# Seven-product couples first in a pair and plain couples last, the second halves' first up chunk in program order, and scratch tiles of their own for the last squares

## The chip, the cores and the metric

The kernel runs on one core of a Trainium2 chip. The metric is the time of one execution on the device, in microseconds (us). The kernel before takes 2386.35 us (median of 3 runs, 2380.95 to 2389.92). An execution under the hardware profiler gives the trace from which all other times come.

Names of the engines: PE is TensorE's matmul, PEld its load of weights, DVE the vector engine, ACT the scalar engine, POOL GpSimd, SP the engine whose queue issues most transfers. PSUM is the memory with 8 banks into which TensorE sums; SBUF is the large on-chip memory; a DMA moves data between the chip's main memory and SBUF.

## The reference, cut to what matters

Two layers over 256 tokens of width 2048. Each is a normed token mixer (an mLSTM in layer 0, an HGRN2 in layer 1) and a normed gated FFN, both added to the stream h. A last norm closes. The change lies in the FFN's second product and in what follows it:

```python
def conv_glu(hn, w_up, conv_w, conv_b, w_down):
    u = hn @ w_up                        # 2048 -> 2 x 5504
    a, v = jnp.split(u, 2, axis=-1)
    ...                                  # c = conv_b + 3-tap convolution of a along the tokens
    return (jax.nn.gelu(c, approximate=False) * v) @ w_down      # 5504 -> 2048

for layer in range(DEPTH):
    ...
    h = h + mix
    h = h + conv_glu(rmsnorm(h, norm_ffn_g[layer]), ...)
return rmsnorm(h, final_g)
```

## The kernel before, in words

**Precision.** The weights lie in main memory as fp32. A piece of 128 x 1024 is loaded ("raw"), split by ACT into a rounded part wh (L149) and by DVE into the rest wl (L150), and every block product is three matmuls: high x high, high x low, low x high. So ACT and DVE work on every weight, and TensorE waits for both.

**The FFN.** Its 5504 hidden columns are worked in two parts per layer, of 22 and 21 blocks of 256 columns: an "up" phase of 22 (21) chunks of some 11 us (matmuls L338 and L342), and then two "pairs", each of which multiplies the whole part into half of the 2048 output columns. After a chunk, done_up (L1184 to L1196) adds up the PSUM banks on ACT and DVE, convolves, applies the GELU and leaves a tile g of 128 hidden columns with its high and low part.

**A pair** (squares_by_seven, matmuls L236) takes two tiles g at a time, a "couple". A plain couple is 24 matmuls on two pieces of weights. A "seven" couple computes the same 2 x 2 blocks by Strassen's scheme with 7 products: 21 matmuls on three and a half pieces. The products P1, P5, P6, P7 collect in four PSUM banks of the pool psm (tag mm, four buffers, the same that the up chunks use), the rest in four banks of pc. The scheme needs sums of blocks of weights (a tile T of 128 x 1536) and sums of tokens (sx). The sums of weights are made ahead, during the up phase, and put into main memory (tscr); in the pair they are loaded (L199), except for one couple, FLY, whose sums DVE makes itself (L208). The sums of tokens are made by token_sums (L564 to L569) as soon as both tiles g are there. SEVEN names the couples of a part that go by seven products.

**What sets the order.** A scheduler fills the engines' queues from priorities and dependencies; what is wrapped in pin or keep_in_program_order stays where it is written. Casts run up to three pieces ahead of the matmuls (LOOK = 3), raw has three buffers. T tiles share the three buffers of the tag avc with the temporaries of done_up. Small work of other stages (norms, preparation of sums) is pushed to a list of side jobs and taken a step at a time.

**End of a pair.** After the last seven couple, mid() (L581 to L589) adds P1, P5, P6, P7 to h, on ACT, DVE and POOL, by way of a scratch tile u of the tag jk, which has one buffer. After the last couple, done() adds the banks pc. In the second part's second pair the last couples run bank by bank (36 matmuls), and each finished bank goes straight to the next norm: to Norm.bank in layer 0, which transposes h on TensorE (L422), and to FinalNorm.bank in layer 1 (L504 to L516), whose last stores end the kernel. Its squares for output block c == 2 run on ACT (L534) and write their unused result to a scratch tile jk.

Of the kernel before, what the change touches and what calls it, by code (L numbers as in the profile page):

```python
# [8 lines left out]
F32 = mybir.dt.float32  # L9
F32R = mybir.dt.float32r  # L10
I32 = mybir.dt.int32
AF = mybir.ActivationFunctionType
# [3 lines left out]
P = 128  # L16
T = 256
# [29 lines left out]
LEAD = 48  # L47
TEMP = 3
GATES = 4 * AH
SEVEN = (1, 2, 3, 4, 5, 6, 7, 8, 9), (1, 2, 3, 4, 5, 6, 7, 8)  # L50
FLY = 5
STORED = 2 * (len(SEVEN[0]) + len(SEVEN[1]) - 2)
BY_TRANSFERS = (9, 27.0), (17, 33.0)
FIRST = 11, 7
# [12 lines left out]
def trunk_kernel(ctx, tc, xT, x_d, fg_d, pp_d, cst_d, w_gate, w_first, w_aq, w_ak, w_av, w_ao, w_aout, w_ao2,  # L67
                 w_bq, w_bv, w_bg, w_bout, w_bo2, w_up, w_d0, w_d1, out, mscr, tscr):
    nc = tc.nc
    act, dve, pool, pe = nc.scalar, nc.vector, nc.gpsimd, nc.tensor  # L70

    keep = ctx.enter_context(tc.tile_pool(name="keep", bufs=1))
# [21 lines left out]
    class Side:  # L94
        def __init__(self):
            self.now, self.jobs, self.behind = 0.0, [], []
# [26 lines left out]
    side, held = Side(), []  # L123


    class Chunk:
        def __init__(self, kind, src, nk, x, done, before=None, swap=(), first=False, paced=False):
            self.swap, self.first, self.paced = swap, first, paced
            self.kind, self.src, self.nk, self.x, self.done, self.before = kind, src, nk, x, done, before
            self.width = {"fm": 256, "tm": 512, "st": 512}[kind]  # L130

    pin = tc.keep_in_program_order
# [90 lines left out]
    def banks():  # L223
        return [psm.tile([P, 512], F32, tag="mm", name="mm") for _ in range(2)]
# [81 lines left out]
    def stream(chunks):  # L306
        pieces = split_weights(chunks)
        ready = []

        def fetch():  # L310
            p = next(pieces, None)
            if p is not None:
                ready.append(p)

        for _ in range(LOOK):
            fetch()
        for ch in chunks:
            if ch.before:
                ch.before()
            if ch.kind == "st":  # L320
                squares_by_seven(ch, fetch, ready)
                continue
            ps = banks()
            k = 0
            while k < ch.nk:
                fetch()
                wh, wl, n = ready.pop(0)
                if ch.kind == "fm":
                    ops = [(kk, f, part) for kk in range(n) for f in range(2) for part in "hl"]
                    for i in ch.swap:  # L330
                        i -= 2 * k
                        if 0 <= i < 2 * n - 1:
                            ops[2 * i + 1:2 * i + 3] = ops[2 * i + 2], ops[2 * i + 1]
                    for kk, f, part in ops:
                        x = ch.x(k + kk)
                        c = kk * ch.width + f * P
                        if part == "h":
                            pe.matmul(ps[f], wh[:, c:c + P], x, start=k + kk == 0, stop=False)  # L338
                            continue
                        if f:  # L340
                            side.tick(0.65)
                        pe.matmul(ps[f][:, 0:T], wl[:, c:c + P], x[:, 0:T], start=False, stop=k + kk == ch.nk - 1)  # L342
                    k += n
                    continue
                for kk in range(n):
                    x = ch.x(k)
                    st, sp = k == 0, k == ch.nk - 1
                    c = slice(kk * 512, (kk + 1) * 512)
                    ops = [(t, i) for t in range(2) for i in range(3)]
                    if ch.first and st:  # L350
                        ops.sort(key=lambda o: (0, 2, 1)[o[1]])
                    for t, i in ops:
                        a, w = ((0, wh), (0, wl), (T, wh))[i]
                        pe.matmul(ps[t], x[:, a + t * P:a + (t + 1) * P], w[:, c], start=st and i == 0, stop=sp and i == 2)  # L354
                    side.tick(1.3)
                    k += 1
            ch.done(ps)
# [112 lines left out]
    class FinalNorm:  # L470
# [5 lines left out]

        def load(self):
            self.g = [keep.tile([P, 512], F32, tag=f"xt{c}", name=f"fg{c}") for c in range(4)]
            for c in range(4):
                pool.dma_start(self.g[c], fg_d[:, c * 512:(c + 1) * 512].broadcast_to([P, 512]))  # L480

        def add(self, c):
            cs = slice(512 * c, 512 * c + 512)
# [15 lines left out]
        def bank(self, ps, i):  # L499
            if i == 0:  # L500
                side.drain()
            t, c = i // 2, 2 + i % 2
            h, total, rc = hm[:, t, 512 * c:512 * c + 512], self.ss[:, t, c:c + 1], self.rc[:, t:t + 1]
            pin(dve.tensor_tensor(h, h, ps, ALU.add))  # L504
            if c == 2:
                square(h, total)
                if t:
                    self.store(0)
                pin(dve.scalar_tensor_tensor(rc, total, 1.0 / D, rc, ALU.mult, ALU.add))
                return  # L510
            last = keep.tile([P, 512], F32, tag=f"xt{4 + t}", name="fl")
            pin(dve.scalar_tensor_tensor(last, h, 1.0, h, ALU.mult, ALU.mult, accum_out=total))
            pin(dve.scalar_tensor_tensor(rc, total, 1.0 / D, rc, ALU.mult, ALU.add))
            pool.tensor_tensor(rc, rc, hmx[:, 0:1], ALU.pow)
            v = hm[:, t, 1024:1536]
            pin(dve.tensor_tensor(v, v, self.g[2], ALU.mult))  # L516
            if t:
                self.store(1)
# [13 lines left out]
    def square(src, total, pin=lambda ins: ins):  # L532
        jk = ev.tile([P, 512], F32, tag="jk", bufs=1, name="jk")
        pin(act.activation(jk, src, AF.Square, accum_out=total))  # L534
# [630 lines left out]
    def ffn(layer, norm, nxt):  # L1165
# [39 lines left out]
        for part, (f0, nf) in enumerate(((0, FA), (FA, FB))):  # L1205
            GT, SX, seven = [], {}, SEVEN[part]

# [7 lines left out]
            for i in range(nf):  # L1215
                chunks.append(Chunk("fm", w_up[layer, f0 + i], KT, norm.x, done_up(f0 + i, i, GT, SX, seven),
                                    prep if i == 0 else None,
                                    swap=((2, 12), (2,))[layer] if part and i == 0 else (3,) if f0 + i == 1 else (), paced=True))

            for c0, src in ((0, w_d0[layer][:, f0 * 1024:(f0 + nf) * 1024]), (2, w_d1[layer][:, f0 * 1024:(f0 + nf) * 1024])):  # L1220
                ch = pair(src, nf, c0, lambda k, GT=GT: GT[k], lambda u, SX=SX: SX[u], nxt if part else None, seven)
                ch.waits = []
                for u in seven:
                    if u != FLY:
                        ch.stored[u] = tscr[box["n"]]
# [23 lines left out]
    nf = FinalNorm()  # L1249
    chunks = mlstm(n0, n1)  # L1250
    c, close0, chunks[6].before = ffn(0, n1, n2)
    chunks += c
    c = hgrn(n2, n3)
    b = c[0].before

    def swap():
        close0()
        b()
    c[0].before = swap
    d, close1, c[1].before = ffn(1, n3, nf)  # L1260
    chunks += c + d
    stream(chunks)
    close1()

# [97 lines left out]
```

## Time and profile before

| what | value |
| --- | --- |
| time, median of 3 runs | 2386.35 us (2380.95 to 2389.92) |
| the profiled execution | 2386.37 us, span 2384.4 us, clock 0.998 |
| TensorE busy | 2361.6 us, 14524 matmuls |
| pairs of layer 0 start at | 639.36, about 695, 986.09, about 1037 us |
| pairs of layer 1 start at | 1925.51, about 1980, 2265.97, about 2318 us |
| last matmul ends, span ends | 2372.17, 2384.4 us |

A row of the timeline gives start, duration, engine, line, operation, output <- inputs; in square brackets stands how long the engine had been idle before it, and what released it. A row of the stages gives a stretch, its length and the busy time of the engines in it. Matmuls overlap, so the time that one costs is the distance between starts (0.227 us for 128 x 512), not its duration.

### The profile page before, as it was taken

To read this page: it belongs to the slowest core of one execution; us is meant where nothing else is said; L and a number is where in the kernel's file an instruction comes from. 1 tells how busy PE (TensorE), PEld (TensorE's weight loads), DVE (VectorE), ACT (ScalarE), POOL (GpSimd) and SP (SyncE) were. 2 spreads that over 40 slices of the span, in tenths; PEclk is the share of its full clock that TensorE was granted. 3 is DMA by queue.
4 is the path that set the end of the run, shared out by engine and by line. 5 is a ranking of instruction groups with operands and counts; after the bars stand their busy time and mean duration, and the time that the engine had idled before them with its cause. 6 is when DMAs were issued, how large, how long until landed. Compare 5 with 4: busy or idle time off the path is not lost.

```text
span 2384.4 us, 38410 instructions
## 1 busy us (share of the span) xinstructions
PE 2361.6 (99%) x14524; PEld 2019.2 (85%) x14524; DVE 1998.9 (84%) x3254; ACT 1393.0 (58%) x2201; POOL 282.4 (12%) x348
## 2 busy tenths in 40 slices
PE   9999999999999999999999999999999999999997
PEld 7888888888888888888888888888888888888876
DVE  7766677988899888898898989889779889888888
ACT  7655455555565555676555555556556576455565
POOL 0110111000000000001333333331010000000000
PEclk9999999999999999999999999999999999999999
DMA  8766878888798888796777777767897788777785
GB/s 299 215 212 232 257 221 274 309 296 289 275 340 305 292 278 280 272 328 219 223 222 232 211 236 222 221 213 235 279 309 274 245 307 325 265 248 243 246 322 203
DMA packets 122986, 624.32 MB, mean 262 GB/s; under 512 B 13856, under 2 KB 14368, under 8 KB 74672
## 3 DMA queue, kind: packets, MB, share of 16 engines
q1 hardware_dynamic: 106128, 590.59, 70.1%
q0 software_dynamic: 16096, 30.48, 8.3%
q8 instruction: 114, 1.87, 0.3%
q10 hardware_dynamic: 576, 0.79, 0.1%
q14 instruction: 72, 0.59, 0.1%
HBM read 584.00 MB, written 92.34 MB: 284 GB/s over the span
## 4 chain that ended last, share of the span: by engine, by line
PE 85%; DVE 5%; DMA 5%; issue 2%; ACT 1%; POOL 1%; SPq 0%; POOLq 0%; DVEq 0%; ACTq 0%
PE mm L338 33%; PE mm L342 17%; PE mm L354 16%; PE pc L236 9%; PE mm L236 7%; DVE wl L150 3%; DMA raw<-in_w_up 1%; DMA T<-tscr 1%; DMA pwh<-in_w_d 1%; DMA raw<-in_w_d 1%; DMA pwl<-in_w_d 1%; PE pn L845 1%; ACT wh L149 1%; PE py L1102 1%; PE pd L1052 0%
## 5 line engine op out<-in xcount | busy, mean ns | idle before, releaser
L338 PE MATMUL mm<-xt,wh 128*128 128x512 f32 x3776 | 1317.9, 394 | 0.0
L150 DVE TENSOR_TENSOR wl<-raw,wh 128x1024 fp32r<-128x1024 f32 (+1 forms) x844 | 1033.7, 1229 | 242.9 <-ACT wh L149 237.0
L149 ACT CAST wh<-raw 128x1024 fp32r<-128x1024 f32 (+1 forms) x844 | 875.2, 1043 | 564.6 <-PE mm L338 295.7
L342 PE MATMUL mm<-xt,wl 128*128 128x256 f32 x3776 | 1051.6, 280 | 1.8 <-issue 1.2
L338 PEld LDWEIGHTS mm<-xt,wh 128*128 128x128 f32 x3776 | 705.8, 187 | 158.9
L342 PEld LDWEIGHTS mm<-xt,wl 128*128 128x128 f32 x3776 | 711.5, 188 | 7.4 <-issue 2.0
L354 PE MATMUL mm<-wh,xt 128*128 128x512 f32 x1024 | 321.7, 393 | 1.8 <-ACT xt L360 1.6
L236 PE MATMUL pc<-wh,g 128*128 128x512 f32 x696 | 237.8, 390 | 0.0
L354 PEld LDWEIGHTS mm<-wh,xt 128*128 128x128 f32 x1024 | 192.1, 188 | 42.2 <-ACT xt L360 2.1
L354 PE MATMUL mm<-wl,xt 128*128 128x512 f32 x512 | 198.7, 392 | 0.0
L236 PE MATMUL mm<-wh,sx 128*128 128x512 f32 x444 | 157.2, 389 | 0.3 <-ACT wh L149 0.3
L149 ACT CAST wh<-T 128x1024 fp32r<-128x1024 f32 (+1 forms) x148 | 122.2, 835 | 55.9 <-DMA T<-tscr 15.6
L236 PEld LDWEIGHTS pc<-wh,g 128*128 128x128 f32 x696 | 130.6, 188 | 27.2
L150 DVE TENSOR_TENSOR wl<-T,wh 128x1024 fp32r<-128x1024 f32 (+1 forms) x148 | 141.5, 967 | 13.1 <-ACT wh L149 12.8
L588 POOL TENSOR_TENSOR hm<-hm,u 128x512 f32<-128x512 f32 x10 | 14.8, 1478 | 1090.4 <-DVE u L587 813.5
L236 PE MATMUL pc<-wl,g 128*128 128x512 f32 x348 | 135.7, 390 | 0.5 <-DVE wl L150 0.5
L354 PEld LDWEIGHTS mm<-wl,xt 128*128 128x128 f32 x512 | 96.6, 189 | 19.1
L1184 ACT COPY avc<-mm 128x256 f32<-128x256 f32 x172 | 64.1, 372 | 69.4 <-PE mm L342 69.4
L236 PEld LDWEIGHTS mm<-wh,sx 128*128 128x128 f32 x444 | 83.2, 188 | 18.0 <-ACT wh L149 0.8
L236 PE MATMUL mm<-wl,sx 128*128 128x512 f32 x222 | 86.6, 390 | 0.6 <-DVE wl L150 0.6
L1189 ACT ACTIVATE avc<-avc,pp 128x256 f32<-128x256 f32 x86 | 51.6, 601 | 57.4 <-DVE avc L1187 57.4
L1185 DVE TENSOR_TENSOR avc<-mm,avc 128x256 f32<-128x256 f32 x172 | 72.2, 420 | 8.6 <-ACT avc L1184 8.4
(248 smaller groups left out, 2444.1 us busy)
## 6 DMA issues: line engine op xcount, KB each, us to landing
raw<-in_w_up SPq DMA_DIRECT2D x172, 1024.0 KB, 5.9
raw<-in_w_bq SPq DMA_DIRECT2D x48, 1024.0 KB, 5.2
raw<-in_w_d SPq DMA_DIRECT2D x60, 768.0 KB, 5.8
T<-tscr SPq DMA_DIRECT2D x60, 768.0 KB, 7.6
tscr<-in_w_d SPq DMA_DIRECT2D x26, 1024.0 KB, 7.5
raw<-in_w_ao SPq DMA_DIRECT2D x24, 1024.0 KB, 6.0
raw<-in_w_d SPq DMA_DIRECT2D x24, 1024.0 KB, 7.0
pwh<-in_w_d SPq DMA_DIRECT2D x36, 512.0 KB, 6.6
```

Source lines behind the costliest of these rows:

```text
L149: pin(act.copy(wh[:, :m], r))
L150: pin(dve.tensor_tensor(wl[:, :m], r, wh[:, :m].bitcast(F32), ALU.subtract))
L236: pin(pe.matmul(ps, a, b, start=id(ps) not in begun, stop=stop and i == 2))
L338: pe.matmul(ps[f], wh[:, c:c + P], x, start=k + kk == 0, stop=False)
L342: pe.matmul(ps[f][:, 0:T], wl[:, c:c + P], x[:, 0:T], start=False, stop=k + kk == ch.nk - 1)
L354: pe.matmul(ps[t], x[:, a + t * P:a + (t + 1) * P], w[:, c], start=st and i == 0, stop=sp and i == 2)
L588: pool.tensor_tensor(part(1, 0), part(1, 0), u, ALU.add)
L845: pe.matmul(pn[:, 0:258], w, v, start=(i == 0), stop=(i == len(parts) - 1))
L1102: pe.matmul(py[:, c], AT[:, s if s == t else 2 + s], V[:, s, j * P:(j + 1) * P], start=(s == 0), stop=(s == 1))
L1184: act.copy(z, p[:, T:2 * T])
L1185: dve.tensor_tensor(z, p[:, 0:T], z, ALU.add)
L1189: act.activation(c, a, AF.Identity, bias=col("conv_b", layer * FT + f), scale=cw[1])
```

## The change

Four edits. The first moves the couples: SEVEN now names couples 0 to 8 of a part of eleven, and 0 to 7 of the other, instead of 1 to 9 and 1 to 8; FLY is couple 4 instead of 5. A pair opens with a product couple and ends with two plain couples, mid() runs a couple earlier, and the sums of tokens are made from the first chunks of an up phase on instead of up to its last ones. The second edit gives the first up chunk of each second part another exchange of neighbouring matmuls (swap), and keeps the matmuls of its first piece in program order (hold). The third turns the final norm's weight loads on POOL (fg) into side jobs of 9.0 steps, in program order. The fourth lets the squares of FinalNorm.bank write a tile sq of their own, in place of the shared jk. Every engine has as many instructions as before.

```diff
-SEVEN = (1, 2, 3, 4, 5, 6, 7, 8, 9), (1, 2, 3, 4, 5, 6, 7, 8)
-FLY = 5
+SEVEN = (0, 1, 2, 3, 4, 5, 6, 7, 8), (0, 1, 2, 3, 4, 5, 6, 7)
+FLY = 4
...
+                    hold = pin if ch.hold and k == 0 else lambda ins: ins
                     for kk, f, part in ops:
...
-                            pe.matmul(ps[f], wh[:, c:c + P], x, start=k + kk == 0, stop=False)
+                            hold(pe.matmul(ps[f], wh[:, c:c + P], x, start=k + kk == 0, stop=False))
...
-                        pe.matmul(ps[f][:, 0:T], wl[:, c:c + P], x[:, 0:T], start=False, stop=k + kk == ch.nk - 1)
+                        hold(pe.matmul(ps[f][:, 0:T], wl[:, c:c + P], x[:, 0:T], start=False, stop=k + kk == ch.nk - 1))
...
         def load(self):
             self.g = [keep.tile([P, 512], F32, tag=f"xt{c}", name=f"fg{c}") for c in range(4)]
+            side.push(self.loads(), True)
+
+        def loads(self):
             for c in range(4):
-                pool.dma_start(self.g[c], fg_d[:, c * 512:(c + 1) * 512].broadcast_to([P, 512]))
+                yield 9.0
+                tc.keep_in_program_order(pool.dma_start(self.g[c], fg_d[:, c * 512:(c + 1) * 512].broadcast_to([P, 512])))
...
             if c == 2:
-                square(h, total)
+                sq = keep.tile([P, 512], F32, tag=f"xt{6 + t}", name="sq")
+                act.activation(sq, h, AF.Square, accum_out=total)
...
-                                    swap=((2, 12), (2,))[layer] if part and i == 0 else (3,) if f0 + i == 1 else (), paced=True))
+                                    swap=(0, 2) if part and i == 0 else (3,) if f0 + i == 1 else (), paced=True,
+                                    hold=part == 1 and i == 0))
```

Lines of the changed kernel stand a few further down: L338 is L339 there, L504 is L509, L509 is L515, and mid()'s L581 to L589 are L587 to L595.

What this does to the queues shows at three places. The first is TensorE's queue at the start of the first pair of all, before the change (mm are banks of psm, pc the other four, g tiles of hidden columns with their numbers, sx sums of tokens):

```order
3044 L236 MATMUL pc<-wh,g_3982 128x512
3045 L236 MATMUL pc<-wl,g_3982 128x512
3046 L236 MATMUL pc<-wh,g_3982 128x512
3047 L236 MATMUL pc<-wh,g_4088 128x512
3048 L236 MATMUL pc<-wl,g_4088 128x512
3049 L236 MATMUL pc<-wh,g_4088 128x512
```

And the same place after it:

```order
3044 L236 MATMUL mm<-wh,g_3982 128x512
3045 L236 MATMUL mm<-wl,g_3982 128x512
3046 L236 MATMUL mm<-wh,g_3982 128x512
3047 L236 MATMUL pc<-wh,g_3982 128x512
3048 L236 MATMUL pc<-wl,g_3982 128x512
3049 L236 MATMUL pc<-wh,g_3982 128x512
3050 L236 MATMUL mm<-wh,sx 128x512
3051 L236 MATMUL mm<-wl,sx 128x512
```

Before, 24 plain matmuls on pc come first; now product P1 on mm stands first, and the first product with a sum of tokens, which needs the first T, is the seventh matmul.

The second is SP's queue of transfers for the same pair, before:

```order
107 L137 DMA raw<-in_w_d 128x2048
108 L137 DMA raw<-in_w_d 128x1536
109 L200 DMA raw<-tscr 128x512
110 L199 DMA T<-tscr 128x1536
111 L137 DMA raw<-in_w_d 128x1536
112 L200 DMA raw<-tscr 128x512
113 L137 DMA raw<-in_w_d 128x1536
114 L200 DMA raw<-tscr 128x512
115 L137 DMA raw<-in_w_d 128x1536
116 L200 DMA raw<-tscr 128x512
117 L199 DMA T<-tscr 128x1536 x3
```

And after:

```order
107 L137 DMA raw<-in_w_d 128x1536
108 L200 DMA raw<-tscr 128x512
109 L137 DMA raw<-in_w_d 128x1536
110 L200 DMA raw<-tscr 128x512
111 L199 DMA T<-tscr 128x1536
112 L137 DMA raw<-in_w_d 128x1536
113 L200 DMA raw<-tscr 128x512
114 L137 DMA raw<-in_w_d 128x1536
115 L200 DMA raw<-tscr 128x512
116 L199 DMA T<-tscr 128x1536 x2
117 L137 DMA raw<-in_w_d 128x2048
```

The raw tile of the plain couple (128x2048, row 107 before) has gone from the front, and the second T stands behind four raw tiles instead of five.

The third is DVE's queue at the end of the last pair, before:

```order
2890 L582 TENSOR_TENSOR hm<-hm,mm 128x512
2891 L150 TENSOR_TENSOR wl<-raw,wh 128x1024
2892 L584 TENSOR_TENSOR hm<-hm,mm 128x512
2893 L586 TENSOR_TENSOR hm<-hm,mm 128x512
2894 L583 TENSOR_TENSOR u<-u,mm 128x512
2895 L585 TENSOR_TENSOR hm<-hm,u 128x512
2896 L587 TENSOR_TENSOR u<-u,mm 128x512
2897 L504 TENSOR_TENSOR hm<-hm,pc 128x512
```

And after:

```order
2873 L588 TENSOR_TENSOR hm<-hm,mm 128x512
2874 L590 TENSOR_TENSOR hm<-hm,mm 128x512
2875 L592 TENSOR_TENSOR hm<-hm,mm 128x512
2876 L150 TENSOR_TENSOR wl<-raw,wh 128x1024
2877 L589 TENSOR_TENSOR u<-u,mm 128x512
2878 L150 TENSOR_TENSOR wl<-raw,wh 128x1024 x2
2879 L591 TENSOR_TENSOR hm<-hm,u 128x512
2880 L593 TENSOR_TENSOR u<-u,mm 128x512
2881 L509 TENSOR_TENSOR hm<-hm,pc 128x512
```

Three subtractions for weights stand among mid()'s six operations instead of one; mid() itself is a couple further from the end of TensorE's work.

More of the change, by code (lines that the diff above doesn't have):

```diff
@@ L126, in trunk_kernel, with __init__ @@
     class Chunk:
-        def __init__(self, kind, src, nk, x, done, before=None, swap=(), first=False, paced=False):
-            self.swap, self.first, self.paced = swap, first, paced
+        def __init__(self, kind, src, nk, x, done, before=None, swap=(), first=False, paced=False, hold=False):
+            self.swap, self.first, self.paced, self.hold = swap, first, paced, hold
             self.kind, self.src, self.nk, self.x, self.done, self.before = kind, src, nk, x, done, before
```

## Prediction

> **What bounds the kernel now.** I read the page first, for the busy engine and the chain that ended last.
>
> ```profile
> span 2384.4 us, 38410 instructions
> PE 2361.6 (99%) x14524; PEld 2019.2 (85%) x14524; DVE 1998.9 (84%) x3254; ACT 1393.0 (58%) x2201; POOL 282.4 (12%) x348
> PE 85%; DVE 5%; DMA 5%; issue 2%; ACT 1%; POOL 1%; SPq 0%; POOLq 0%; DVEq 0%; ACTq 0%
> ```
>
> TensorE is busy for 2361.6 of 2384.4 us, and 85% of the chain that ended last is its own work. The change removes no matmul, so only moments in which TensorE waits, and the tail behind its last matmul, can change the time. All of it lies in the four parts where the FFN's second products run (two "pairs" each). The second view is the table by stage: the first pair cut in two, the first pair of layer 1, and the last two pairs. Columns: PE, PEld, DVE, ACT and POOL busy, granted clock, DMA share, GB/s.
>
> ```profile
> 639.36:650.00 10.64, 10.64 (x49) 8.59 (x47) 5.93 (x12) 4.48 (x9) 0.00 (x0) 1.00 0.84 327
> 650.00:694.00 44.00, 43.24 (x187) 34.63 (x187) 42.40 (x47) 33.35 (x39) 0.00 (x0) 1.00 0.90 339
> 1925.51:1980.00 54.49, 54.49 (x243) 45.09 (x242) 49.77 (x59) 39.86 (x48) 0.89 (x1) 1.00 0.93 348
> 2265.97:2318.00 52.03, 51.87 (x230) 42.58 (x228) 44.02 (x54) 33.48 (x42) 0.45 (x1) 1.00 0.91 331
> 2318.00:2372.20 54.20, 52.26 (x228) 42.64 (x228) 50.74 (x63) 34.36 (x45) 6.53 (x4) 1.00 0.59 215
> ```
>
> The clock is full, so no part of the time is the clock's. Inside a pair DVE is busy for 42.40 of 44.00 us and the DMA engines for 0.90 of the time: both are close behind TensorE. The first 10.64 us of a pair, where today a plain couple (24 matmuls on two pieces of weights) stands, are its only slack: DVE 5.93 us.
>
> The third view is the timeline of TensorE around the places where it stopped.
>
> ```profile
> 649.60 0.62 PE L236 MATMUL mm<-wh,sx 128*128 128x512 f32 x2
> 650.41 0.50 PE L236 MATMUL mm<-wh,g 128*128 128x512 f32 x1 [0.19 <-ACT wh L149]
> 664.05 0.50 PE L236 MATMUL pc<-wl,g 128*128 128x512 f32 x1 [0.54 <-DVE wl L150]
> 1088.22 0.55 PE L422 MATMUL mm<-cst,hm 128*128 128x128 f32 x3 [1.28 <-DVE u L587]
> 2314.55 2.00 ACT L149 CAST wh<-raw 128x1024 fp32r<-128x1024 f32 x2 [4.26 <-DMA raw<-in_w_d]
> 2319.34 0.50 PE L236 MATMUL mm<-wh,g 128*128 128x512 f32 x1 [1.50 <-ACT wh L149]
> 2320.88 0.50 PE L236 MATMUL mm<-wl,sx 128*128 128x512 f32 x1 [0.57 <-DVE wl L150]
> ```
>
> There is little to win: 0.19 in the first pair, 0.54 at the couple whose sums DVE makes itself (L208), 1.28 where the next norm's transposes want a PSUM bank that DVE's L587 of mid() has yet to read, and 1.50 + 0.57 at the start of the last pair. The last has its cause five us earlier: ACT stood 4.26 us for a weight transfer and started late. The fourth view is the timeline of the tail.
>
> ```profile
> 2368.43 1.30 POOL L589 TENSOR_TENSOR hm<-hm,u 128x512 f32<-128x512 f32 x1
> 2369.77 0.63 ACT L534 ACTIVATE jk<-hm 128x512 f32<-128x512 f32 x1 [7.54 <-POOL hm L589]
> 2370.52 0.16 DVE L509 SCALAR_TENSOR_TENSOR fss<-fss 128x1 f32<-128x1 f32 x1 [2.82 <-ACT jk L534]
> 2370.60 0.68 DVE L504 TENSOR_TENSOR hm<-hm,pc 128x512 f32<-128x512 f32 x1
> 2371.78 0.39 PE L236 MATMUL pc<-wh,g 128*128 128x512 f32 x1
> 2375.34 0.68 DVE L504 TENSOR_TENSOR hm<-hm,pc 128x512 f32<-128x512 f32 x1
> ```
>
> The last matmul ends at 2372.17 (2371.78 + 0.39), but DVE takes the last bank only at 2375.34. Behind it come 9.06 us of closing work and stores to 2384.4. DVE is late because the first square waits for POOL's L589: the square writes a scratch tile (tag jk) whose one buffer L589 still reads as u.
>
> **The change, part by part.** The profiled execution took 2386.37 us, span 2384.4, which is the median (2386.35) but for 0.02; the sum is made against it.
>
> *Last squares.* With tiles of their own, and with mid() one couple of 24 matmuls (5.4 us) earlier, the first square waits for nothing but its bank. The tail is 36 matmuls bank by bank at 0.227 us (in the timeline one starts every 0.227), so bank 2 of 4 is complete 18 matmuls, 4.08 us, before 2372.17, at 2368.09. From its L504 to that of the fourth bank the order on DVE and ACT is kept: 2375.34 - 2370.60 = 4.74 us. So the fourth L504 starts near 2368.24 + 4.74 = 2372.98, with 0.15 for the handover: **-2.4**. It cannot be better than 3.1 (TensorE's end). It is nothing if mid() now makes DVE late for the first banks.
>
> ```profile
> 2317.38 1.22 DVE L150 TENSOR_TENSOR wl<-raw,wh 128x1024 fp32r<-128x1024 f32 x1
> 2317.55 2.19 POOL L588 TENSOR_TENSOR hm<-hm,u 128x512 f32<-128x512 f32 x1 [58.66 <-DVE u L587]
> 2318.51 2.31 DVE L150 TENSOR_TENSOR wl<-T,wh 128x1024 fp32r<-128x1024 f32 x1
> ```
>
> That mishap has a row: beside POOL's L588 a subtraction of 1.22 us took 2.31, and the add 2.19 instead of 1.30. In the tail today the two adds run beside bank sums at 1.30; now they run beside subtractions. Price on DVE 2 x 1.09 = 2.2 us, within two couples (10.9 us of TensorE) that ask DVE for four subtractions (4.9) and mid()'s six operations (4.1, by the 0.68 of an L504 of the same shape): 11.2, a third of a us too much, but up to three pieces are cast ahead. The two orders of DVE in the tail, shown with the change, say the same: mid() still comes last ahead of the banks, with three subtractions in it instead of one. I take 0. The Trainium skill (SBUF — State Buffer, Who interferes with whom) says that a DVE instruction with two SBUF inputs contends with a GpSimd one that reads SBUF, and that one with a single SBUF input does not; the trace agrees (2.31 against 1.22, and 1.30 beside sums that read PSUM). By that rule alone the tail's gain would shrink by those 0.3, to -2.1.
>
> *mid() one couple earlier.* The PSUM banks of the products come free before the next norm's transposes ask for them: **-1.28** at 1088.22. At 2317 the two plain couples at the end need 2 pieces each where the seven-product couple before needed 3.5, so loads of the next pair come through earlier: **-2.07**, or nothing if the transfers themselves were the limit there (DMA share 0.91). The 0.19 of the first pair goes, the 0.54 moves with its couple and stays: **-0.19**.
>
> *Seven-product couples first.* Now the price. The two orders of TensorE at the first pair, shown with the change, open with three plain matmuls on bank pc before, and with three of a product on bank mm now. So products stand where 24 plain matmuls stood. The second sum tile T, which today is asked for after 24 + 21 matmuls, is asked for at the 28th matmul here and at the 33rd at the other three starts (counted in the order of TensorE). The rows around it now:
>
> ```profile
> 639.36 0.39 PE L236 MATMUL pc<-wh,g 128*128 128x512 f32 x1
> 641.06 0.42 DVE L1185 TENSOR_TENSOR avc<-mm,avc 128x256 f32<-128x256 f32 x1
> 641.39 0.68 DVE L150 TENSOR_TENSOR wl<-T,wh 128x512 fp32r<-128x512 f32 x1
> 642.10 0.99 SPq L199 DMA_DIRECT2D T<-tscr  x2
> 648.36 1.05 ACT L149 CAST wh<-T 128x1024 fp32r<-128x1024 f32 x1 [2.83 <-DMA T<-tscr]
> 649.32 1.04 ACT L149 CAST wh<-raw 128x1024 fp32r<-128x1024 f32 x1
> DMA to landing us min/median/max: 6.2/6.8/7.4
> ```
>
> T takes one of three buffers that it shares with the last chunks' temporaries, so its load is issued (642.10) when DVE has finished the wl before it. In the new order L1193 and L1185 stand behind that wl, so the issue moves from 642.10 to about 640.8, no earlier than 640.3 (with the other wl too) and no later than 642.1. Plus 6.2 and a cast of 1.05: 648.05. TensorE asks at 639.36 + 27 x 0.227 = 645.5. Stall 2.55; the raw piece cast behind T in ACT's order (649.32, a step of 0.96) is asked for two matmuls (0.45) later: 0.5 more. **+3.0**; bounds, with 4.2 (below) from 640.3 and 7.4 from 642.1: 0 to 5.6. For the other three starts the landings of the T loads in the first tens of us, and the first issue, are (986.09, 1925.51 and 2265.97, in this order):
>
> ```profile
> L199 SPq DMA_DIRECT2D T<-tscr x9: 319/320/451, 985.7 to 1025.3; - x9
> DMA to landing us min/median/max: 4.2/7.8/9.0
> L199 SPq DMA_DIRECT2D T<-tscr x2: 319/319/319, 1925.2 to 1928.9; - x2
> DMA to landing us min/median/max: 4.2/5.2/6.3
> L199 SPq DMA_DIRECT2D T<-tscr x5: 319/320/428, 2267.5 to 2289.9; - x5
> DMA to landing us min/median/max: 5.5/8.0/9.3
> ```
>
> The 33rd matmul comes 32 x 0.227 = 7.3 us after the start. At 986 I take the middle of the landings: 985.7 + 6.6 + 1.05 = 993.4, just in time: **0** (bounds 0 to 2.4). At 1925: 1925.2 + 5.2 + 1.05 = 1931.5, needed at 1932.8: **0** (0 to 2.5 with the 9.0 of 986). At 2266 the load waits for less in the new order than now (SP's queue only), so I put it a us earlier, 2266.5 + 7.4 + 1.05 = 2275.0 against 2273.3, and take two thirds, since the rest of that stretch has the lowest DVE load: **+1.2** (0 to 4.6).
>
> PSUM is not late: the product banks 3 and 4 wait for DVE's two L1185, which ended by 642.41, and are asked for at the 22nd and 25th matmul, 644.1 and 644.8. The sums of the last couples leave the end of each up phase, about 2.0 us of DVE, and enter its beginning, in steps of 0.29 us under chunks of some 11:
>
> ```profile
> L564 DVE TENSOR_TENSOR avc<-avc x136: 279/292/295, 453.7 to 2241.7; 128x128 f32<-128x128 f32 x136
> L480 POOL DMA_DIRECT2D fg<-in_fg x4: 536/546/615, 2256.0 to 2258.4; - x4
> ```
>
> *Up chunk kept in order, and the norm weights' loads.* At 750 and 2035 TensorE goes from pair to chunk without a wait now; a pinned order with another swap costs 0, covered by pieces cast ahead; uncovered it would be one cast, 1.05, at each of two places. The fg loads hold POOL 0.55 us each, the fourth now between two pairs' adds; DVE wants them 70 us later: 0.
>
> **Sum:** -2.4 - 1.3 - 2.1 - 0.2 = -6.0; +3.0 + 0 + 0 + 1.2 = +4.2; net -1.8: 2384.5 us.
>
> **Rivals.** (a) *The loads land in time everywhere.* Against it are the 6.2 and 8.0 above, for it the 4.2. Then only the gains count: 2386.4 - 6.0 = 2380. The Trainium skill (DMA: Bandwidth & Descriptors, Anatomy of one DMA) gives about 2.0 us and 436 GB/s for a DMA of its software path; for T's 786 KB an estimate of 3.8 us, and by it the first T would be cast at 645.7 and nothing would stall. No landing quoted here was that short.
> (b) *T starves all four starts: slower.* One mechanism: the shared buffer is freed late and the load stands behind the raw pieces on the same busy engines. At the long landings: 640.8 + 9.0 + 1.05 - 645.5 + 0.5 = 5.9 (9.0 seen at 986), 2.4, 2.5 and 4.6, together 15.4; minus 6.0: 2395.8. It decides from landings of 3.7, 6.7, 6.6 and 4.8 us on, in the order of the starts (the time asked for, less the cast and the issue), where each further us costs a us. If DVE, at 42.40 of 44.00 us, cannot catch up afterwards and the 2.1 at 2319 isn't won either, 2398.
> (c) *The gains move instead of going*: the 2.1 at 2319 (transfers at 0.91 are the limit) and the tail (DVE late from the slow subtractions) stay, and the starts cost 4.2: 2386.4 - 1.5 + 4.2 = 2389.
>
> **Chances.** Forecast 0.43, (a) 0.27, (b) 0.15, (c) 0.15. The range takes in (a) with the tail's 3.1 and (b) at its price: 2377 to 2395.5; the forecast's own is 2381 to 2388. A measurement here can tell about 0.5% (12 us) from no change, so nearly all of this is "no change": faster than 2374.4 would need twice the gains found, 0.05; slower than 2398.3 is (b) without the 2.1, 0.07; the same 0.88.
>
> **What would show it.** Right: TensorE waiting for ACT's wh, and ACT for T<-tscr, some 6 us behind 639 and little of it at 986 and 1925; no wait for L593 near 1088; the last bank's L509 about 0.8 us behind TensorE's end. Wrong: TensorE without a wait in the first 12 us of all four pairs (then a), waits over 2 us at 986 and 1925 (then b), or ACT's square still behind POOL's L595 or the start of the last pair still waiting 2 us (then c).

## The result, and the profile after

The changed kernel takes 2378.88 us (median of 20 runs, 2373.34 to 2387.07); the kernel before, on the same chip, 2385.78 (20 runs, 2380.82 to 2395.82). The ratio is 0.9972, with a 95% interval of 0.9962 to 0.9982: 6.7 us less, between 4.3 and 9.1. It is a small gain, under the 0.5% that the prediction took for the least that a measurement can tell; with 20 runs of each the interval is 0.1% to either side, so the gain is told from no change. It is larger than the 1.8 us of the forecast. The profiled execution took 2383.29 us, span 2381.3, so it is one of the slower ones of its kernel by 4.4 us; the two traces can't be subtracted as wholes, only place by place.

The page of the changed kernel, the lines that answer to those of before:

```profile
span 2381.3 us, 38367 instructions
PE 2361.4 (99%) x14524; PEld 2016.8 (85%) x14524; DVE 1998.7 (84%) x3254; ACT 1392.0 (58%) x2201; POOL 283.8 (12%) x348
PE 88%; DMA 4%; DVE 4%; issue 2%; ACT 1%; POOL 1%; SPq 0%; POOLq 0%; DVEq 0%; ACTq 0%
```

TensorE's busy time is what it was. The waits at the pairs, from TensorE's timeline of the changed kernel (the first pair begins at 638.02, the first of layer 1's second part at 2264.46, the last one near 2316.5):

```profile
644.56 0.73 PE L236 MATMUL mm<-wh,sx 128*128 128x512 f32 x2 [0.23 <-ACT wh L149]
645.51 0.50 PE L236 MATMUL pc<-wh,g 128*128 128x512 f32 x1 [0.21 <-ACT wh L149]
2273.21 0.50 PE L236 MATMUL mm<-wl,sx 128*128 128x512 f32 x1 [0.24 <-DVE wl L150]
2345.64 0.50 PE L236 MATMUL mm<-wh,g 128*128 128x512 f32 x1 [1.17 <-ACT wh L149]
```

The 1.28 us at the norm's transposes and the 1.50 + 0.57 at the start of the last pair are gone, and the 0.54 at the couple whose sums DVE makes is 0.16. A wait of 1.17 stands in the middle of the last pair instead, in this execution. At the start of the first pair TensorE waits 0.44 us, where the forecast had 3.0. The tail:

```profile
2366.19 0.63 ACT L512 ACTIVATE sq<-hm 128x512 f32<-128x512 f32 x1 [7.37 <-DVE hm L509]
2367.51 0.69 DVE L509 TENSOR_TENSOR hm<-hm,pc 128x512 f32<-128x512 f32 x1 [0.40 <-PE pc L236]
2371.16 0.39 PE L236 MATMUL pc<-wh,g 128*128 128x512 f32 x1
2372.26 0.68 DVE L509 TENSOR_TENSOR hm<-hm,pc 128x512 f32<-128x512 f32 x1
```

The square now waits for its bank's sum alone, and the last bank is taken 0.71 us behind TensorE's last matmul (2371.55), where it was 3.17. From the last matmul to the end are 9.75 us instead of 12.21.

These add up to some 6 us less, with 0.7 of new waits at the starts and 1.2 in the last pair. Layer 1's first up phase has three waits in this execution (0.60, 0.40 and 1.56 us), where before it had one of 0.48. What I had not looked at is the pace of the up phases where they have no waits. The table by stage shows it: two stretches of 200 us inside the up phases of the two second parts, and 100 us of layer 1's first part, before:

```profile
770.00:970.00 200.00, 200.00 (x1134) 173.40 (x1133) 171.04 (x281) 110.19 (x175) 0.00 (x0) 1.00 0.83 283
1810.00:1910.00 100.00, 100.00 (x579) 88.19 (x578) 84.74 (x138) 56.04 (x91) 0.00 (x0) 1.00 0.73 248
2050.00:2250.00 200.00, 200.00 (x1156) 174.83 (x1155) 168.02 (x271) 111.53 (x179) 0.00 (x0) 1.00 0.73 248
```

And of the changed kernel:

```profile
770.00:970.00 200.00, 200.00 (x1156) 174.88 (x1155) 173.01 (x283) 113.64 (x181) 0.00 (x0) 1.00 0.84 286
1810.00:1910.00 100.00, 100.00 (x568) 86.86 (x568) 82.98 (x135) 55.77 (x91) 0.00 (x0) 1.00 0.72 242
2050.00:2250.00 200.00, 200.00 (x1156) 174.90 (x1155) 167.31 (x269) 112.14 (x180) 0.00 (x0) 1.00 0.73 247
```

TensorE is busy for all of each stretch, at a granted clock of 1.00, and still gets through 1134 matmuls in one stretch of 200 us and 1156 in another. A chunk's matmuls alternate between 512 and 256 columns, so that is 200 / 567 = 353 ns for a pair of matmuls against 200 / 578 = 346. A second part's up phase has 21 x 32 = 672 such pairs: 4.5 us. Layer 0's second part ran at the slow pace before and at the fast one now. Layer 1's first part (1810 to 1910) was fast before and is slow in this execution: 579 and 568 in 100 us.

### The profile page after: what moved, and what is told of

The parts are those of the page before. It is cut to its first block, busy times and chain, and to the rows that moved or that the text cites. A ratio compares the mean times of both kernels' runs of the same rounds, so it can differ in the third digit from the quotient of the medians.

```text
span 2381.3 us, 38367 instructions
## 1 busy us (share of the span) xinstructions
PE 2361.4 (99%) x14524; PEld 2016.8 (85%) x14524; DVE 1998.7 (84%) x3254; ACT 1392.0 (58%) x2201; POOL 283.8 (12%) x348
## 4 chain that ended last, share of the span: by engine, by line
PE 88%; DMA 4%; DVE 4%; issue 2%; ACT 1%; POOL 1%; SPq 0%; POOLq 0%; DVEq 0%; ACTq 0%
PE mm L339 33%; PE mm L343 17%; PE mm L355 16%; PE pc L236 11%; PE mm L236 7%; DVE wl L150 2%; DMA T<-tscr 1%; DMA raw<-in_w_up 1%; DMA pwh<-in_w_d 1%; PE pn L851 1%; ACT wh L149 1%; PE py L1108 1%; PE pd L1058 0%; DMA pwl<-in_w_d 0%; PE pa L1058 0%
## 5 line engine op out<-in xcount | busy, mean ns | idle before, releaser
L339 PE MATMUL mm<-xt,wh 128*128 128x512 f32 x3776 | 1318.4, 396 | 0.4 <-issue 0.4
L339 PEld LDWEIGHTS mm<-xt,wh 128*128 128x128 f32 x3776 | 707.8, 188 | 161.7 <-issue 0.7
```

Of the source, the lines that this page charges most:

```text
L339: hold(pe.matmul(ps[f], wh[:, c:c + P], x, start=k + kk == 0, stop=False))
```

## Experiments

**Two theories.** M: how an up phase begins decides its pace, and the second edit, which I had costed at nothing, brings 4.5 us that way; the couples and the tail bring the rest. N: the second edit does nothing, as predicted, and the moved couples carry the whole gain.

**The second edit undone in the changed kernel.**

```diff
-                                    swap=(0, 2) if part and i == 0 else (3,) if f0 + i == 1 else (), paced=True,
-                                    hold=part == 1 and i == 0))
+                                    swap=((2, 12), (2,))[layer] if part and i == 0 else (3,) if f0 + i == 1 else (), paced=True))
```

> The changed kernel with its second edit undone: the first up chunk of each second part has its old exchanges and is not kept in program order, all else stays. Theory M (the start of an up phase decides its pace): in the changed kernel the up phase of layer 0's second part runs at about 347 ns for a pair of matmuls (128x512 and 128x256), in the kernel before at 353; the start of the chunk sets this for all 21 chunks. Undoing the edit puts one or both second up phases at another start, and if at the slow pace it costs 660 x 6.6 ns = 4.3 us each: 2383 to 2388 us, ratio to the kernel before 0.999 to 1.001. Theory N (the couples and the tail make the gain, the edit costs and brings nothing, as predicted): ratio 0.997, and 347 ns in both phases.

Measured: 2384.20 us (12 runs), ratio 0.9986 (0.9975 to 0.9997), 3.3 us over the changed kernel's ratio; the two intervals overlap, so the count of matmuls says more here. The two second up phases:

```profile
770.00:970.00 200.00, 200.00 (x1134) 173.46 (x1133) 170.48 (x279) 111.35 (x175) 0.00 (x0) 1.00 0.83 280
2050.00:2250.00 200.00, 200.00 (x1156) 174.91 (x1155) 167.37 (x270) 112.58 (x180) 0.00 (x0) 1.00 0.73 248
```

One phase is slow, layer 0's, as M has it, and the other is not.

**The couples alone, on the kernel before.**

```diff
-SEVEN = (1, 2, 3, 4, 5, 6, 7, 8, 9), (1, 2, 3, 4, 5, 6, 7, 8)
-FLY = 5
+SEVEN = (0, 1, 2, 3, 4, 5, 6, 7, 8), (0, 1, 2, 3, 4, 5, 6, 7)
+FLY = 4
```

> The kernel before with only the couples moved (SEVEN and FLY), everything else as before. Theory M: it gets what the trace shows for the couples (1.45 us at the norm's transposes, 2.4 at the start of the last pair, less about 1.9 of new waits), 2 us, and the pace of the two second up phases is that of the kernel without the second edit: 2379 to 2388 us, a ratio of 0.999 if one phase is slow. Theory N: the moved couples carry most of the 7 us: ratio 0.998 with no change of pace.

Measured: 2386.45 us (12 runs), ratio 0.9992 (0.9980 to 1.0004): 1.9 us less, with an interval that takes in zero. Layer 0's second up phase stays slow (1133 matmuls from 770 to 970). The interval ends at 4.8 us, so the couples alone don't carry 6.7 us, as N has it. The tail of its trace is worth a look. Its span, and its last lines of ACT, DVE and TensorE:

```profile
span 2383.8 us, 38369 instructions
2368.93 0.63 ACT L534 ACTIVATE jk<-hm 128x512 f32<-128x512 f32 x1 [7.64 <-POOL hm L589]
2369.98 0.69 DVE L504 TENSOR_TENSOR hm<-hm,pc 128x512 f32<-128x512 f32 x1
2373.64 0.39 PE L236 MATMUL pc<-wh,g 128*128 128x512 f32 x1
2374.73 0.68 DVE L504 TENSOR_TENSOR hm<-hm,pc 128x512 f32<-128x512 f32 x1
```

The square waits for POOL still, on the shared scratch tile, but with mid() a couple earlier POOL is done in time, and the last bank follows the last matmul by 0.70 us, as in the changed kernel, without the squares' own tiles.

**The squares' own tiles alone, on the kernel before.**

```diff
-                square(h, total)
+                sq = keep.tile([P, 512], F32, tag=f"xt{6 + t}", name="sq")
+                act.activation(sq, h, AF.Square, accum_out=total)
```

> The kernel before with only the squares' own scratch tile. By the rows of before the second bank's sum need not wait for the first square: the fourth bank's sum would start near 2373.3 instead of 2375.3 on that trace (DVE ends mid() at 2367.0, so not all of the gain of the changed kernel). Both theories: the tail from the last matmul to the end 2 us shorter, 12.2 to about 10.2, ratio 0.999; pace of the up phases as in the kernel before.

Measured: 2387.11 us (11 runs), ratio 1.0000 (0.9991 to 1.0010). In its trace the tail is 11.26 us (its last matmul starts at 2374.45), so 0.95 us shorter instead of 2. The timeline tells why: the tile is no longer in the way, the adds on POOL are.

```profile
2371.10 1.30 POOL L590 TENSOR_TENSOR hm<-hm,u 128x512 f32<-128x512 f32 x1
2371.15 1.26 DVE L510 SCALAR_TENSOR_TENSOR fss<-fss 128x1 f32<-128x1 f32 x1 [0.79 <-ACT sq L507]
2372.34 0.67 DVE L504 TENSOR_TENSOR hm<-hm,pc 128x512 f32<-128x512 f32 x1
```

A DVE operation on 128 x 1 takes 1.26 us beside POOL's add, where it takes 0.16 in the traces of before and after: 1.10 us more, about what is missing of the 2. It is the slowing of the prediction's 2.31 us row, in a place where I had counted none.

**The second edit alone, on the kernel before** (couples, squares and loads as before):

```diff
-                                    swap=((2, 12), (2,))[layer] if part and i == 0 else (3,) if f0 + i == 1 else (), paced=True))
+                                    swap=(0, 2) if part and i == 0 else (3,) if f0 + i == 1 else (), paced=True,
+                                    hold=part == 1 and i == 0))
```

> The kernel before with only the second edit: first up chunk of each second part with exchanges 0 and 2 and its first piece in program order. Theory M: the up phase of layer 0's second part goes from about 353 to 347 ns for a pair of matmuls, 4.3 us: 2381.5 us, ratio 0.998. Theory N: nothing, as predicted (0 us), ratio 1.000.

Measured: 2382.07 us (12 runs), ratio 0.9983 (0.9969 to 0.9997): 4.1 us less, from the edit that was to do nothing. Its second up phase of layer 0:

```profile
770.00:970.00 200.00, 200.00 (x1156) 174.90 (x1155) 172.34 (x284) 112.64 (x180) 0.00 (x0) 1.00 0.84 286
```

M holds: 4.1 us by the times, 4.5 by the count of matmuls. The other traces agree: layer 0's second up phase begins fast in all seven kernels that have exchanges 0 and 2 there, and is slow in all five that don't have them.

**Order or exchange?** The edit does two things: it keeps the chunk's first piece in program order, and it exchanges neighbours at places 0 and 2. This kernel keeps the order and drops the exchange:

```diff
-                                    swap=(0, 2) if part and i == 0 else (3,) if f0 + i == 1 else (), paced=True,
+                                    swap=() if part and i == 0 else (3,) if f0 + i == 1 else (), paced=True,
```

> The changed kernel with the first up chunk of each second part still in program order, but without exchanges: its matmuls alternate (512, 256, 512, 256) from the first on, where the changed kernel starts 512, 512, 256, 256 twice. If the exchanges decide the pace: 353 ns for a pair of matmuls in one or both second up phases, 4.3 us each, 2383 to 2388 us, ratio 0.999 to 1.001. If only the unbroken order decides (nothing of the pair between the chunk's matmuls): 347 ns in both, 2379 us, ratio 0.997.

Measured: 2385.52 us (12 runs), ratio 1.0008 (0.9994 to 1.0021), so 8.6 us over the changed kernel's ratio, about two times 4.5. Both second up phases are slow:

```profile
770.00:970.00 200.00, 200.00 (x1134) 173.36 (x1133) 170.41 (x281) 111.22 (x176) 0.00 (x0) 1.00 0.83 281
2050.00:2250.00 200.00, 200.00 (x1134) 173.40 (x1133) 163.85 (x264) 110.28 (x176) 0.00 (x0) 1.00 0.72 245
```

So the unbroken order alone does not bring the fast pace; the exchanges do: two matmuls of 512 columns and then two of 256, twice at the start, against plain alternation. Whether they need the order too, no kernel here shows.

The trace of the couples alone tells more of the old exchanges, which stood at places 2 and 12 in layer 0 and at 2 alone in layer 1. In layer 0 the distances between the starts of 128x512 matmuls go to 350 and 343 ns in turn behind the exchange at place 2, and to 351, 361, 349 behind the one at place 12; in layer 1 they stay at 350 and 343. So the slow pace of layer 0's second part came with its exchange at place 12, and the changed kernel no longer has that one.

**An exchange in every chunk.**

```diff
-                                    swap=(0, 2) if part and i == 0 else (3,) if f0 + i == 1 else (), paced=True,
+                                    swap=(0, 2) if part or i else (3,) if f0 + i == 1 else (), paced=True,
```

> The changed kernel with exchanges 0 and 2 in every up chunk but the first two of a layer. In the profiles so far the first up phase of each layer ran at 347 ns in some runs and at 353 in others, and went to 353 behind a wait in the middle (the changed kernel near 1708, the one with the second edit alone in the same phase), never back. If each exchange sets the pace anew, all four phases run at 347 in every run from a chunk behind such a wait: median 2375 to 2377 us (0 to 2 slow phases of 4.3 us saved), ratio 0.9955, and less scatter. If the exchange only works at the start of a phase: 2379, ratio 0.997. If the exchange itself costs, slower.

Measured: 2378.27 us (12 runs), ratio 0.9971 (0.9957 to 0.9984), no better than the changed kernel. In its trace layer 1's first up phase is fast until a wait of TensorE of 1.45 us that ends at 1775.4, and slow from there to its end, through some twelve chunks that each begin with the two exchanges (all but the first chunk of a layer have them, not all but two as the expectation says) (first stretch ahead of the wait, second behind it, 55 us each):

```profile
1710.00:1765.00 55.00, 55.00 (x319) 48.10 (x318) 45.08 (x78) 31.41 (x52) 6.62 (x8) 1.00 1.00 330
1800.00:1855.00 55.00, 55.00 (x313) 47.67 (x313) 46.05 (x75) 29.91 (x48) 0.00 (x0) 1.00 0.74 250
```

The expectation that each exchange sets the pace anew fell. Exchanges 0 and 2 together keep whichever pace there is; a wait can change it. They cost nothing.

**Which start does what?** One kernel with single chunks of the four phases begun in other ways, all kept in program order (the chunk's number, and its exchanges; -1 stands for the eight 512-column matmuls of the first piece ahead of the eight of 256):

```diff
+STARTS = ({4: (0,), 7: (0,), 10: (1,), 13: (1,), 16: (2,), 19: (2,)},
+          {3: (-1,), 6: (-1,), 9: (0,), 12: (-1,), 15: (2,), 18: (0, 2)},
+          {4: (0,), 6: (-1,), 9: (2,), 11: (-1,), 14: (1,), 16: (-1,), 19: (0, 2)},
+          {3: (2,), 6: (0,), 9: (2,), 12: (1,), 15: (-1,), 18: (-1,)})
...
+                    if ch.swap == (-1,) and k == 0:
+                        ops.sort(key=lambda o: o[2] == "l")
```

> The changed kernel with other starts for single up chunks inside the four phases, kept in program order (one exchange at place 0, 1 or 2; exchanges 0 and 2; or all eight 512-column matmuls of the first piece ahead of its eight of 256), to see which of them moves the pace between 347 and 353 ns for a pair of matmuls, and which way. If the pace is a state that a single exchange turns over, it alternates at the marked chunks. If only a wait or a pair before the chunk can set it, every phase keeps its pace from its start to its end. If the run of eight sets it like the 512-column matmuls of a pair do, each such chunk brings the same pace, from either side. One exchange is one slow or fast chunk each 11 us; no time is forecast beyond 2373 to 2390 us.

Measured: 2382.20 us (one run). Its first phase, 15 us from ahead of chunk 4, behind 4, behind 7 and behind 10:

```profile
420.00:435.00 15.00, 15.00 (x89) 13.08 (x88) 14.88 (x28) 9.50 (x17) 0.00 (x0) 1.00 0.94 321
450.00:465.00 15.00, 15.00 (x87) 12.97 (x86) 12.20 (x22) 9.73 (x17) 0.00 (x0) 1.00 0.94 336
485.00:500.00 15.00, 15.00 (x89) 13.12 (x88) 13.72 (x25) 7.42 (x12) 0.00 (x0) 1.00 0.78 260
520.00:535.00 15.00, 15.00 (x87) 12.98 (x86) 12.99 (x21) 7.97 (x12) 0.00 (x0) 1.00 0.80 274
```

The pace turns at each marked chunk, 89 matmuls and 87 in turn; by the starts of the single matmuls it is 347, 353, 347, 353 ns for a pair, and so on to the end of the phase. Over the whole kernel 12 of 15 single exchanges turned the pace over, both pairs of exchanges left it as it was, and all eight runs of eight left the slow pace behind them, four of them coming from the fast one (the next expectation says seven, a miscount). Of the three single exchanges that did not turn it, two stood in a slow stretch (chunk 14 of layer 1's first phase, chunk 6 of its second) and one in a fast one (chunk 4 of layer 1's first phase, 346.7 ns ahead of it and 346.8 behind).

**A reset, to win what is left.** From this I made a version that was to end fast from any start: a run of eight to force the slow pace, then a single exchange to turn it, in the first phase of each layer.

```diff
+STARTS = {2: (-1,), 3: (2,)}, {}, {3: (-1,), 4: (2,), 10: (-1,), 11: (2,)}, {}
...
+                    if ch.swap == (-1,) and k == 0:
+                        ops.sort(key=lambda o: o[2] == "l")
```

> The changed kernel with a reset in the first up phase of each layer: one chunk (2 in layer 0; 3 and again 10 in layer 1) opens with its eight 512-column matmuls ahead of the eight of 256, which left the slow pace behind it in all seven cases tried, and the next chunk has the single exchange at place 2, which turned slow to fast in four of four cases. If that holds, both phases end at 347 ns for a pair of matmuls from any start: a phase that began slow saves up to 4 us, a chunk run slow on purpose costs 32 x 6.6 ns = 0.2 us; median 2376 to 2378 us, ratio 0.996, and fewer runs over 2382. If the exchange does not hold from that state, the phases end slow in every run: 2384 us and more.

Measured: 2383.68 us (11 runs, 2381.45 to 2384.59), ratio 0.9987 (0.9977 to 0.9997): worse than the changed kernel. Both first phases end slow:

```profile
430.00:630.00 200.00, 200.00 (x1134) 173.34 (x1133) 172.65 (x289) 112.15 (x180) 0.00 (x0) 1.00 0.84 288
1810.00:1910.00 100.00, 100.00 (x567) 86.67 (x567) 81.74 (x131) 54.77 (x89) 0.00 (x0) 1.00 0.73 242
```

The exchange directly behind the run of eight did not turn the pace, as the expectation's other case had it. The starts of the single matmuls, read afterwards, show where it stood. At the slow pace the distances from one 128x512 matmul to the next go 350, 361, 349 ns over and over. Nine single exchanges of the kernel before this one and all three of this one were made at that pace. The seven that turned it follow a distance of 349 or 350; the five that didn't, this kernel's three among them, follow the 361. No further run tests this reading. It would mean that the reset failed by the place of its exchange, and not because a run of eight can't be undone.

It is a failure that tells something else too: with both phases slow in the trace, the runs lie within 3.1 us, while those of the changed kernel spread over 13.7. That much of this spread is first up phases that fall into one pace or the other is a guess. The profiled run of the late sums below, fast in all four phases, took 2380.07 us and that of the reset, slow in both first phases, 2382.18; of the other runs there is no trace.

**The mis-sized wait at the first pair.** I had costed the token sums that leave the end of an up phase at nothing. This kernel puts operations of their shapes back there, on scratch that nothing reads:

```diff
                     SX[i // 2] = token_sums(mp, n, box["c"], c, avc[:, 0:2 * T], z)
+                elif i % 2 and i // 2 == len(seven):
+                    S, b = avc[:, 0:2 * T], box["c"]
+                    for o in range(4):
+                        dve.tensor_tensor(S[:, o * P:(o + 1) * P], c[:, P:T], b[:, P:T], ALU.subtract)
+                    dve.tensor_tensor(S[:, 0:384], avc[:, 0:384], avc[:, 128:512], ALU.subtract)
+                    dve.tensor_tensor(S[:, 384:512], c[:, 0:P], b[:, 0:P], ALU.subtract)
```

> The changed kernel with six more DVE operations of about 2 us (the shapes of one couple's sums of tokens, on scratch that nothing reads afterwards; the result is the same) at the place where the kernel before made its last sums, two or three chunks ahead of each first pair. Theory: the second T could be loaded before the first pair began because these 2 us had left DVE; with them back, the wl that frees its buffer ends later, the load goes out 1 to 3 us later than in the changed kernel (637.2, 0.8 us ahead of the pair's first matmul), and TensorE waits 1.5 to 3 us at the first pair instead of 0.8. Rival: the load is held by something else, and the wait stays at 0.8. Time: 0 to 4 us over the changed kernel.

Measured: 2379.65 us (10 runs), ratio 0.9976 (0.9963 to 0.9989), which can't be told from the changed kernel's 0.9972; the place itself can. The load of the second T and TensorE's wait, first in the changed kernel (pair from 638.02), then here (from 639.0):

```profile
637.21 1.58 SPq L199 DMA_DIRECT2D T<-tscr  x2
```

```profile
640.62 0.81 SPq L199 DMA_DIRECT2D T<-tscr  x2
648.06 0.73 PE L236 MATMUL mm<-wh,sx 128*128 128x512 f32 x2 [2.78 <-ACT wh L149]
```

With the six operations put back (1.73 us of DVE, between 625.14 and 628.83), the load goes out 1.6 us behind the start of the pair instead of 0.8 ahead of it, and TensorE waits 2.78 us instead of 0.23. That is the prediction's figure (1.44 behind the start, 2.55). The way to it is not the time on DVE alone. The operations work in an avc tile, and T shares the buffers of that tag. The load of the pair's first T, first in the changed kernel, then here, with the last of the six operations and DVE's first work on that T:

```profile
624.78 0.37 SPq L199 DMA_DIRECT2D T<-tscr  x1
```

```profile
628.55 0.28 DVE L1213 TENSOR_TENSOR avc<-avc 128x128 f32<-128x128 f32 x1
628.86 0.32 SPq L199 DMA_DIRECT2D T<-tscr  x1
636.11 1.23 DVE L150 TENSOR_TENSOR wl<-T,wh 128x1024 fp32r<-128x1024 f32 x1 [2.15 <-DMA raw<-tscr]
```

The first T's load goes out 0.03 us behind the end of the last of the six, 10.1 us ahead of the pair instead of 13.2. ACT casts this T 6.2 us later, at 635.03, and DVE stands idle for 2.15 us before it takes it up (the row names another transfer as what ended that). The wl that frees the buffer of the second T then ends at 640.54, where it ended at 637.19 in the changed kernel.

**The third and fourth edits undone in the changed kernel**, the shared scratch tile and the four loads of the norm's weights together:

```diff
-            side.push(self.loads(), True)
...
-                sq = keep.tile([P, 512], F32, tag=f"xt{6 + t}", name="sq")
-                act.activation(sq, h, AF.Square, accum_out=total)
+                square(h, total)
```

> The changed kernel with the third and fourth edits undone: the last squares write to the shared scratch tile again, and the four loads of the norm's weights go out together. The kernel with only the couples moved had a tail of 9.73 us behind the last matmul, the one with only the own tiles 11.26, the one before 12.21. So the earlier mid() brings all of it: tail 9.7 to 9.8, time as the changed kernel, ratio 0.997. If the own tiles are needed in this order, 10.5 and more.

Measured: 2375.29 us (7 runs), ratio 0.9963 (0.9948 to 0.9979), against 0.9972 (0.9962 to 0.9982) with both edits. The intervals overlap, so it is no worse; that it is better isn't shown. Its tail is 9.84 us (last matmul from 2369.46, span 2379.7), so the two edits are worth 0.1 us there.

## Why the prediction was right and wrong, step by step

The forecast was no change that a measurement here can tell by its 0.5%, 2384.5 us within 2377 to 2395.5. The time, 2378.88, lies in that range, but outside the forecast's own 2381 to 2388. In size it is rival (a) that came, 2380, and its sign too, but for the 0.44 and 0.24 us that TensorE waits at two of the four starts. That is luck in part: by the separate kernels some 4 of the 6.7 us come from an edit that the prediction and (a) both put at 0.

- **The tail, -2.4.** Measured 12.21 to 9.75: -2.46. The amount was right and the cause was not. I put it down to the squares' own tiles and mid() together. Alone the tiles shorten the tail by 0.95 and move no median (1.0000); the earlier mid() alone gives 9.73 us.
- **The norm's transposes, -1.28, and the last pair's start, -2.07.** Both waits are gone. In the changed kernel's trace 1.17 us came back in the middle of the last pair. Of the nine kernels with the couples in this order, three have such a wait in their trace (0.90 to 1.20), so it comes and goes.
- **The second T at the first pair, +3.0.** This step failed: 0.44 was measured (0.23 + 0.21). The landing (6.2 us) and the matmul that asks were right. What failed was the issue time: the wl that frees the buffer was put at 640.8, by moving two small operations behind it, and the sums that leave the end of the phase were costed at nothing two paragraphs later. That wl ended at 637.19. With operations of the sums' shapes put back the waits there are 2.78 + 0.22, since they keep a buffer from the first T and so put off the second.
- **The other starts, 0, 0 and +1.2.** No wait of TensorE at the start of the pairs at 980 and 1924; 0.24 us near 2273 instead of 1.2. With the couples alone it was 0.96 + 0.23, and 0.74 + 0.24 with the late sums, so the 1.2 was possible.
- **"A pinned order with another swap costs 0."** This step failed, and it is the larger half of the result. I looked for waits of TensorE around 750, found none, and stopped. Behind it stands a wrong premise at the head of the prediction, that with no matmul removed only waits and the tail can change the time. The pace of the matmuls behind the chunk's start was slow by 6.7 ns a pair for 233 us, with TensorE busy throughout. Undoing the edit costs 3.3 us by the ratios, the edit alone brings 4.1, and the count of matmuls gives 4.5.

By the separate kernels the couples bring 1.9 us and the second edit 4.1: 6.0, against 6.7 for all four edits. The sums agree within their intervals. The other two edits show no gain of their own.

## What to carry to other kernels

A stage that shows no waits is not therefore at its best pace: count the matmuls of equal stretches in equal stages, and where two stages of the same code differ by a per cent or two, look at how each begins. When work leaves a place, ask which queue it stood in, which buffer it kept, and what was behind it there: two microseconds "under cover" can be exactly what held a load. And take a gain that two edits share apart before crediting one of them.

## What the runs showed of the hardware

I had not expected that the same sequence of matmuls, alternating 512 and 256 columns, runs at two paces, 346.7 and 353.3 ns for a pair by the distance of their starts, both at a granted clock of 1.00 in the stages and with TensorE busy throughout. The fast pace shows as 343 and 350 ns in turn, and behind some waits as 346, 347, 347; the slow one as 350, 361, 349. A pace survives from chunk to chunk. It can be turned by one exchange of neighbours (12 of 15 in one kernel, none of three in the reset), set to slow by a run of eight matmuls of 512 columns followed by eight of 256 (eight of eight), and turned by a wait of TensorE. In the changed kernel it turned behind this row; waits of 0.40 and 1.56 us later in the same phase left it as it was:

```profile
1709.65 0.39 PE L343 MATMUL mm<-xt,wl 128*128 128x256 f32 x1 [0.60 <-DVE wl L150]
```

In two traces (the squares' own tiles alone, and the old tail) layer 0's first phase turns slow at its chunk 3 with no wait of TensorE. Why there are two paces stays open. The weight loads show no reason: between 770 and 970 us they start 1 to 5 ns behind a matmul's start and last 186 to 190 ns, before and after alike.

The other thing is how much a POOL add can slow DVE beside it: a subtraction went from 1.22 to 2.31 us, and an operation on 128 x 1 from 0.16 to 1.26. The Trainium skill (SBUF — State Buffer, Who interferes with whom) says that a DVE instruction with two SBUF inputs contends with a GpSimd instruction that reads SBUF, and calls the port pair that they share an exclusive lock. The trace agrees: the operation on 128 x 1 begins 0.05 us behind an add of 1.30 us and ends with it.
